# A decoder layer on one core: every engine's order written anew, one order over all engines, and norm rows stored once per partition

## The chip, the core and the metric

The kernel runs on one core of a Trainium2 chip. Five engines each work through a queue of their own, strictly in its order: PE (TensorE, matrix products), DVE (VectorE), ACT (ScalarE), POOL (GpSimd) and SP (SyncE, which here only issues transfers). An instruction that waits holds up everything behind it in its queue. The metric is device time in microseconds (us) of one execution. What a measurement of this kernel can tell from no change is about 0.2%, 1.64 us.

## The reference

One post-norm decoder layer for x of 512 tokens by 1024 channels, all in float32:

```python
h = x @ w_in                              # one projection, cut into 13 parts
y_a = nsa_attention(q, kc, vc, ks, vs, kw, vw, gates, ...) @ w_nsa_out
y_b = gated_deltanet(qkv, beta, decay, gate, ...) @ w_gdn_out
mix = (sigmoid(gate_a) * y_a + sigmoid(gate_b) * y_b) @ w_o
x = layer_norm(ALPHA * x + mix, ln1_g, ln1_b)
h = causal_dwconv(x @ w_up, conv_w)       # 2 x 2816 channels, width 3
gate, val = split(h)
x = layer_norm(ALPHA * x + (silu(gate) * val) @ w_down, ln2_g, ln2_b)
```

The attention has three branches (compressed blocks, the best eight of the selected blocks, a sliding window) with a gate each; the DeltaNet works in chunks of 64 tokens, with a triangular solve for each chunk. `layer_norm(x, g, b)` is `(x - mean) * rsqrt(var + eps) * g + b` over the 1024 channels.

## The kernel before, in words

**Products.** Float32 accuracy comes from splitting every operand in two: ACT (or DVE or POOL) makes a rounded copy, DVE (or POOL) the rest. A weight block arrives by a transfer as `raw`, becomes `wh` and `wl`, and every product is three matrix products into the same PSUM bank: hi by hi, lo by hi, hi by lo (lines L481, L483, L484; L1285 and L1449 are the same for the output projection and the FFN's second product, L536 to L538 for the token-major part of the first projection). A weight tile serves 128x512 outputs. `raw`, `wh` and `wl` have three buffers each, so a transfer can be issued only when an older block has been split.

**Stages.** Up to about 20 us PE makes the token-major projection `pb` out of x and its weights as they arrive (`xr`, `wB`). Then, to about 320 us, the other projections (`gps`) are mixed with attention (`aps`, `pout`) and DeltaNet (`dps`, the solve L769, L770, L772 on DVE). From there to 420 us come the two mixers' output projections, `pm0` and `pm1`: L1196 multiplies each by its gate `mt` (a tanh of a `gps`, L1118 on ACT), L1198 adds the two, and L1176, L1177 and L1210 to L1214 split the sum and make the sums of a two-by-two block product. To 460 us the projection `w_o` (L1285, into `pw` and `pu`), with L1290 adding it to x, L1249 and L1250 the norm, L1262 transposes. To about 715 us the FFN's up products (`pu`), the convolution (L1404, L1407) and the gate (L1411 to L1413), whose result is split into `ph` and `pl` (L1417, L1423, L1418, L1424) and added up in `sr` (L1425 to L1427). The down products (L1449) run to 812 us, as seven block products whose left sides are sums, copied by ACT to `hs` (L1443) and by DVE to `sl` (L1444). L1482 and L1486 take them off PSUM, then the norm again, and the result is sent out.

**Order.** `QUEUES` holds, for each engine, the numbers of its instructions as the program makes them, in the order in which they are to stand. `queues(tc)` walks each list and adds a scheduling dependency between neighbours on the same engine: no wait on the chip, only a place. Between engines nothing is fixed; the framework puts in what semaphores the data need, and which buffer or PSUM bank a rotating tile takes follows from the order in which it sees the instructions.

**Norm rows.** `layout` stacks the four rows g and b of both norms to 4 x 1024 (`lnr`). `rows_of(t, o)` at L1230 issues a transfer of two rows from SP into 128 partitions, reading the same 8 KB for each partition. `ln1` is read first by L1249 at 448 us, `ln2` at 792 us.

Of the kernel before, what the change touches and what calls it, by code (L numbers as in the profile page):

```python
# [19 lines left out]
D = 1024  # L20
# [50 lines left out]
def layout(a):  # L71
# [18 lines left out]
    for i in range(8):  # L90
# [28 lines left out]
        "lnr": np.stack([g("ln1_g")[0], g("ln1_b")[0], g("ln2_g")[0], g("ln2_b")[0]]),  # L119
# [207 lines left out]
77 81 87 90 110 78 71 84 72-73 70 93 85 74 92 94 86 82 91 95 111 144 96-97 83 98-99 79 100 106 101-102 89 103 112-130  # L327
132 131 133-137 147 150 138-139 142-143 145 153 148 146 149 151-152 154-155 157 156 158-161 163 162 165 164 166-171""",
    "SP": """0-7 17 8-9 15 25 10 12 11 13-14 19 18 16 20-24 26-75 80 79 81-82 78 83 77 84-85 76 86-134 136-165 167 135 169 171
173-180 170 166 182 168 172 181 183-184""",  # L330
}


# [1235 lines left out]
```

## Time and profile before

| | |
|---|---|
| time of three runs | 819.83, 820.98, 821.59 us; median 820.98 |
| span of the profiled execution | 820.8 us, mean granted PE clock 0.998 |
| busy: PE, DVE, ACT, POOL | 98%, 73%, 50%, 22% of the span |
| the chain that ended last | PE 79%, DVE 9%, DMA 7%, ACT 2%, issue 2% |
| the transfers of the norm rows | 2 of 1024 KB, issued at 429.6 and 775.4 us; issue to landing 9.6 and 6.7 us |

The page gives no time of its own for the profiled execution beside this span, which is 0.2 us under the median of the runs; sums that start at the span are therefore carried over to the median as they are. In a row of the timeline stand the start, the duration, the engine, the line, the operation, the tiles written and read, their shape, a count of like neighbours (xN), and in brackets the idle time before it and what ended it. Matrix products overlap, so that the step from one start to the next (0.223 us for 128x512 in steady stretches) says what one costs, not its duration.

### The profile page before, as it was taken

The numbers are of one execution on the slowest core, as the hardware profiler recorded it, in microseconds if no ns is written. First come the engines' busy times: TensorE is split into PE (matmuls) and PEld (weight loads), VectorE is DVE, ScalarE is ACT, GpSimd is POOL, SyncE is SP. The second block draws the span as 40 slices with busy tenths as digits, with TensorE's granted clock in tenths as the row PEclk, the third lists the DMA queues.
The fourth block names the chain that finished last, engine by engine and source line by source line (L and its number), as shares of the span: only waits on it lengthen the run. The fifth ranks groups of instructions, "written<-read, shape, count | busy, mean of one in ns | idle before, by whom it ended". The sixth has DMA issues, their size and how long they took to land.

```text
span 820.8 us, 11781 instructions
## 1 busy us (share of the span) xinstructions
PE 802.4 (98%) x4138; PEld 670.2 (82%) x4138; DVE 600.2 (73%) x1339; ACT 409.1 (50%) x912; POOL 179.7 (22%) x176
## 2 busy tenths in 40 slices
PE   8999999999999999999999999999999999999996
PEld 8788888787888888888787898888888888878784
DVE  5667689979768965556578956666685667777888
ACT  4453587774577764323254234344354444565641
POOL 0244835042365111241200101111111210200000
PEclk9999999999999999999999999999999999999999
DMA  8327280013624942343357387285336492465674
GB/s 282 106 78 267 80 267 30 26 53 97 161 86 103 194 90 77 108 134 123 103 209 226 129 168 243 93 185 146 98 117 210 111 235 91 143 202 178 210 220 149
DMA packets 43978, 119.57 MB, mean 146 GB/s; under 512 B 3472, under 2 KB 4624, under 8 KB 43664
## 3 DMA queue, kind: packets, MB, share of 16 engines
q1 hardware_dynamic: 32144, 87.37, 33.3%
q0 software_dynamic: 11776, 31.46, 16.6%
q8 instruction: 32, 0.52, 0.3%
q14 instruction: 26, 0.21, 0.1%
HBM read 116.72 MB, written 33.55 MB: 183 GB/s over the span
## 4 chain that ended last, share of the span: by engine, by line
PE 79%; DVE 9%; DMA 7%; ACT 2%; issue 2%; SPq 0%; POOL 0%; DVEq 0%; ACTq 0%; POOLq 0%
PE pu L481 9%; PE pu L483 9%; PE pu L484 9%; PE gps L481 9%; PE gps L483 8%; PE gps L484 8%; DMA raw<-wsum 3%; PE pout L1086 2%; PE aps L1072 2%; DMA raw<-in_down 2%; DVE wl L1385 2%; PE pz L1449 2%; PE pm L483 2%; PE pm L481 2%; PE pm L484 2%
## 5 line engine op out<-in xcount | busy, mean ns | idle before, releaser
L471 DVE TENSOR_TENSOR wl<-raw,wh 128x512 fp32r<-128x512 f32 x146 | 103.9, 717 | 73.2 <-ACT wh L467 40.9
L467 ACT ACTIVATE wh<-raw 128x512 fp32r<-128x512 f32 x126 | 79.0, 629 | 138.6 <-PE pu L483 91.4
L484 PE MATMUL pu<-mh,wl 128*128 128x512 f32 (+1 forms) x384 | 129.9, 372 | 0.2 <-DVE wl L471 0.2
L481 PE MATMUL pu<-mh,wh 128*128 128x512 f32 (+1 forms) x384 | 129.8, 372 | 0.0
L483 PE MATMUL pu<-ml,wh 128*128 128x512 f32 (+1 forms) x384 | 129.6, 372 | 0.0
L481 PE MATMUL gps<-xh,wh 128*128 128x512 f32 x320 | 123.5, 399 | 2.4 <-ACT mt L1118 1.5
L483 PE MATMUL gps<-xl,wh 128*128 128x512 f32 x320 | 123.2, 397 | 0.0
L484 PE MATMUL gps<-xh,wl 128*128 128x512 f32 x320 | 122.8, 397 | 0.0
L484 PEld LDWEIGHTS pu<-mh,wl 128*128 128x128 f32 x384 | 71.3, 188 | 13.4 <-DVE wl L471 0.6
L481 PEld LDWEIGHTS pu<-mh,wh 128*128 128x128 f32 x384 | 71.0, 188 | 12.6
L483 PEld LDWEIGHTS pu<-ml,wh 128*128 128x128 f32 x384 | 71.0, 188 | 12.6
L1407 DVE SCALAR_TENSOR_TENSOR fa<-pu,fcw,fa 128x511 f32<-128x511 f32 (+1 forms) x88 | 64.9, 745 | 18.9 <-ACT fa L1404 18.3
L1413 POOL TENSOR_TENSOR fth<-fth,fa 128x512 f32<-128x512 f32 x22 | 31.3, 1428 | 197.3 <-DVE fth L1412 182.8
L481 PEld LDWEIGHTS gps<-xh,wh 128*128 128x128 f32 x320 | 60.0, 188 | 13.5 <-issue 2.9
L484 PEld LDWEIGHTS gps<-xh,wl 128*128 128x128 f32 x320 | 60.0, 188 | 11.0 <-POOL wl L471 0.2
L483 PEld LDWEIGHTS gps<-xl,wh 128*128 128x128 f32 x320 | 60.1, 188 | 10.6
L1384 ACT ACTIVATE wh<-raw 128x512 fp32r<-128x512 f32 x67 | 40.0, 625 | 37.2 <-DMA raw<-wsum 11.4
L1385 DVE TENSOR_TENSOR wl<-raw,wh 128x512 fp32r<-128x512 f32 x67 | 44.5, 691 | 15.8 <-ACT wh L1384 15.3
L1404 ACT ACTIVATE fa<-pu,fcw 128x512 f32<-128x512 f32 x44 | 29.5, 681 | 30.7 <-PE pu L484 29.2
L471 POOL TENSOR_TENSOR wl<-raw,wh 128x512 fp32r<-128x512 f32 x30 | 40.0, 1337 | 13.5 <-ACT wh L467 7.1
L522 POOL TENSOR_TENSOR rs<-rs,minus_half 128x1 f32<-128x1 f32 x8 | 7.6, 949 | 155.9 <-DVE rs L1243 103.2
L1045 ACT ACTIVATE sc<-sc,mn 128x384 f32<-128x384 f32 (+2 forms) x64 | 35.6, 558 | 5.7 <-DVE mn L1043 5.2
(365 smaller groups left out, 1702.1 us busy)
## 6 DMA issues: line engine op xcount, KB each, us to landing
raw<-in_up SPq DMA_DIRECT2D x44, 512.0 KB, 3.7
raw<-in_wT SPq DMA_DIRECT2D x40, 512.0 KB, 3.5
wsum<-in_down POOLq DMA_DIRECT2D x6, 2816.0 KB, 21.7
raw<-wsum SPq DMA_DIRECT2D x20, 512.0 KB, 4.3
raw<-in_down SPq DMA_DIRECT2D x15, 512.0 KB, 3.9
osum<-in_wo POOLq DMA_DIRECT2D x6, 1024.0 KB, 9.4
wsum<-wsum POOLq DMA_DIRECT2D x2, 2816.0 KB, 14.2
raw<-in_wm SPq DMA_DIRECT2D x8, 512.0 KB, 3.5
```

Source lines behind the costliest of these rows:

```text
L467: A.activation(wh, r, AF.Copy)
L471: eng.tensor_tensor(wl, r, wh.bitcast(F32), op=OP.subtract)
L481: i = PE.matmul(ps, wh[k], mh_(k), start=(k == 0), stop=False)
L483: PE.matmul(ps, wh[k], ml_(k), start=False, stop=False)
L484: PE.matmul(ps, wl[k], mh_(k), start=False, stop=(k == n - 1))
L1045: A.activation(s[:, i, :n], s[:, i, :n], AF.Exp, scale=-1.0, bias=mn[:, 0, i:i + 1], accum_out=mn[:, 1, i:i + 1])
L1072: PE.transpose(pt[:, i, k, :], s[:, i, k * 128:(k + 1) * 128], ident)
L1384: A.activation(hi, raw[:, i], AF.Copy)
L1385: V.tensor_tensor(lo, raw[:, i], hi.bitcast(F32), op=OP.subtract)
L1404: A.activation(acc, ps, AF.Copy, scale=w[:, 2:3])
L1407: V.scalar_tensor_tensor(acc[:, n:], ps[:, :S - n], w[:, i:i + 1], acc[:, n:], op0=OP.mult, op1=OP.add)
L1413: G.tensor_tensor(th, th, g[1], op=OP.mult)
```

## The change

`lnr` is stored 128 times, once for each partition, and `rows_of` reads it so. All five lists in `QUEUES` are written anew. A string `TURNS` gives one order over all engines (P, D, A, G for POOL, S; a number repeats the letter), which `queues` adds as a second chain of scheduling dependencies. The instructions themselves are the same ones; most stand within 3 us of their old place, a few up to 12 us away. Through `TURNS` 577 of 1678 tiles take another buffer or PSUM bank than before.

```diff
+import re
...
-        "lnr": np.stack([g("ln1_g")[0], g("ln1_b")[0], g("ln2_g")[0], g("ln2_b")[0]]),
+        "lnr": np.broadcast_to(np.stack([g("ln1_g")[0], g("ln1_b")[0], g("ln2_g")[0], g("ln2_b")[0]]), (128, 4, 1024)),
...
 QUEUES = {
-    "PE": """0-9 11-12 10 13-32 41 38 35-37 33 42-43 53 39 34 54 44-45 47-48 40 50-52 46 49 59 62 55 63 65 56 64 60 66-67 61 57-58
...
+TURNS = """DS3P2SPS3DSADSASPDSP3ASP3ASDP2SDPAPSDP2DSP3SP2SP3SAP3SP2DPAP2ADP2DP3AP5DPAP2AP2DP3DPAP3APDP3APDP3AP3AP5DP2AP2DP3DP5DP3
...
 def queues(tc):
...
+    def chain(items):
+        for a, b in zip(items, items[1:]):
+            tc.add_manual_dep(b, a.name, mybir.DependencyInfo(
+                mybir.DependencyClass.NoSync, mybir.DependencyReason.SCHED_ONLY), reason="place in its queue")
+
+    rows = {}
     for k, runs in QUEUES.items():
-        last = None
-        for run in runs.split():
...
+        ends = [r.partition("-")[::2] for r in runs.split()]
+        rows[k] = [made[k][n] for a, b in ends for n in range(int(a), int(b or a) + 1)]
+        chain(rows[k])
+    names = {"G" if k == "Pool" else k[0]: iter(r) for k, r in rows.items()}
+    chain([next(names[x]) for x, n in re.findall(r"([A-Z])(\d*)", TURNS) for _ in range(int(n or 1))])
...
     def rows_of(t, o):
-        nc.sync.dma_start(out=t, in_=bass.AP(tensor=d["lnr"].tensor, offset=d["lnr"].offset + o * D,
-                                             ap=[[0, 128], [D, 2], [1, D]]))
+        nc.sync.dma_start(out=t, in_=d["lnr"][:, o:o + 2, :])
```

Lines from 332 on of the old file stand 54 or 55 further down in the new one: L1285 is L1339 there, L484 is L539, L1182 is L1237. Three places show the kind of move.

**PE at about 395 us** (old clock): the end of a pair `pm0`, `pm1`, then the gate product `gps_4659` that takes the PSUM bank of an older gate product. Before:

```order
L481 MATMUL gps_4566<-xh_93,wh_4562 128x512
L484 MATMUL pm0_4603<-yoh_4005,wl_4597 128x512
L483 MATMUL gps_4566<-xl_94,wh_4562 128x512
L484 MATMUL pm1_4617<-yoh_4005,wl_4601 128x512
L484 MATMUL gps_4566<-xh_93,wl_4564 128x512
L481 MATMUL gps_4566<-xh_93,wh_4562 128x512
L483 MATMUL gps_4566<-xl_94,wh_4562 128x512
L484 MATMUL gps_4566<-xh_93,wl_4564 128x512
L481 MATMUL gps_4659<-xh_93,wh_4651 128x512
```

Now:

```order
L539 MATMUL pm1_4617<-yoh_4005,wl_4601 128x512
L538 MATMUL gps_4566<-xl_94,wh_4562 128x512
L539 MATMUL gps_4566<-xh_93,wl_4564 128x512
L536 MATMUL gps_4566<-xh_93,wh_4562 128x512
L538 MATMUL gps_4566<-xl_94,wh_4562 128x512
L539 MATMUL gps_4566<-xh_93,wl_4564 128x512
L536 MATMUL gps_4566<-xh_93,wh_4562 128x512
L538 MATMUL gps_4566<-xl_94,wh_4562 128x512
L539 MATMUL gps_4566<-xh_93,wl_4564 128x512
L536 MATMUL gps_4566<-xh_93,wh_4562 128x512
L538 MATMUL gps_4566<-xl_94,wh_4562 128x512
L539 MATMUL gps_4566<-xh_93,wl_4564 128x512
```

The pair is finished first; eleven products of `gps_4566` now stand between its last product and `gps_4659` (the next row), where four stood.

**PE at about 419 us:** the end of the last pair, and the first product into `pu1_4886`, which may start only when DVE has read both `pm` banks (L1196). Before:

```order
L484 MATMUL pm1_4792<-yoh_4005,wl_4776 128x512
L1285 MATMUL pw1_4858<-woh_4209,mh_3997 128x512
L1285 MATMUL pw0_4857<-woh_4209,mh_3997 128x512
L484 MATMUL pm0_4778<-yoh_4005,wl_4772 128x512
L1285 MATMUL pw0_4857<-wol_4210,mh_3997 128x512
L1285 MATMUL pw1_4858<-wol_4210,mh_3997 128x512
L1285 MATMUL pw0_4857<-woh_4209,ml_3998 128x512
L1285 MATMUL pw0_4857<-woh_4209,mh_3997 128x512
L1285 MATMUL pw1_4858<-woh_4209,ml_3998 128x512
L1285 MATMUL pu1_4886<-woh_4390,mh_3997 128x512
```

Now:

```order
L1339 MATMUL pw1_4858<-woh_4209,mh_3997 128x512
L536 MATMUL pm1_4792<-yoh_4005,wh_4774 128x512
L538 MATMUL pm1_4792<-yol_4036,wh_4774 128x512
L539 MATMUL pm0_4778<-yoh_4005,wl_4772 128x512
L539 MATMUL pm1_4792<-yoh_4005,wl_4776 128x512
L1339 MATMUL pu1_4886<-woh_4390,mh_3997 128x512
L1339 MATMUL pu1_4886<-wol_4391,mh_3997 128x512
L1339 MATMUL pu1_4886<-woh_4390,ml_3998 128x512
L1339 MATMUL pu0_4885<-woh_4390,mh_3997 128x512
```

Between the last product of `pm1_4792` and the first of `pu1_4886` stood eight products; now none. On DVE both L1196 (first that of `pm1_4792`, then that of `pm0_4778`) still stand in this order.

**ACT at about 325 us:** the copies `yoh` of both mixers' results, and the first weight block `wh_4114` of the first pair `pm0`. Before:

```order
L1182 ACTIVATE yoh_4005<-oT_3216 128x512
L1182 ACTIVATE yoh_4005<-yT_1416 128x512
L1118 ACTIVATE mt_3974<-gps_3949 128x512
L1182 ACTIVATE yoh_4005<-oT_1504 128x512
L1182 ACTIVATE yoh_4005<-oT_2255 128x512
L467 ACTIVATE wh_4114<-raw_4112 128x512
L467 ACTIVATE wh_4118<-raw_4112 128x512
```

Now:

```order
L1237 ACTIVATE yoh_4005<-oT_3216 128x512
L1237 ACTIVATE yoh_4005<-oT_1504 128x512
L1237 ACTIVATE yoh_4005<-yT_2131 128x512
L1173 ACTIVATE mt_3974<-gps_3949 128x512
L1237 ACTIVATE yoh_4005<-oT_2255 128x512
L1237 ACTIVATE yoh_4005<-yT_1416 128x512
L1237 ACTIVATE yoh_4005<-oT_3700 128x512
L1237 ACTIVATE yoh_4005<-yT_2629 128x512
L522 ACTIVATE wh_4114<-raw_4112 128x512
```

Three more copies stand ahead of the weight block; on PE its first product `pm0_4122` has moved ahead of four products of `gps` that stood before it.

On SP the transfer of `ln1` has moved behind the next three weight blocks (`raw_5045`, `raw_5063`, `raw_5099`), that of `ln2` behind the next two (`raw_7920`, `raw_7950`); at the start the small constants stand behind the blocks of x and `wB`, and `xr5` stands before `xr7`, `wB3` and `xr6`.

More of the change, by code (lines that the diff above doesn't have):

```diff
@@ L328 @@
[L328 to L331 removed]
+    "PE": """0-2 11 14 17-18 15 12 8 3-4 19 9 29 10 5 13 30 20-21 23 6 16 24 22 26-28 7 31 25 35 38 41 32 42 39 36 33 43 34 37
+53-54 44 47 45 40 46 55 50 65 51-52 48-49 59 66 56 60 57 62-63 58 68 64 74 61 67 77 75 71 69 76 72-73 78-79 70 80-81
@@ new lines @@
+3748 3735 3739-3740 3752 3741 3749 3737 3745 3753 3750 3746 3757 3747 3754 3738 3755 3742 3758 3756 3743 3760 3744
+3759 3763 3761-3762 3766 3764-3765 3769-3771 3775-3777 3767 3781 3768 3782 3772 3783 3787 3773-3774 3778 3788
+3779-3780 3784-3786 3790 3789 3791-3793 3796-3798 3802-3806 3794 3807 3795 3799-3801 3808-3821 3847 3822-3828
+3848-3851 3829-3831 3852-3854 3832 3855 3833-3835 3856 3836-3837 3857 3838-3839 3858 3840-3846 3859-3879""",
+    "DVE": """0-2 4-5 3 7 6 9 8 10-15 17 16 18 58-59 19 60-61 20 27 21-23 64 25 90 66 31-32 65 33-41 62 42-43 67 44-45 63 46-47 72
@@ new lines @@
+1231 1236 1218 1237 1222 1220 1240-1241 1228 1232 1224 1242 1223 1233 1243 1238 1248 1225 1244 1249-1250 1229 1245
+1251-1252 1254 1246 1253 1239 1255 1234 1256-1257 1235 1258 1247 1259-1262 1265 1263-1264 1266-1270 1273 1271-1272
+1274""",
+    "Activation": """0-1 3-4 2 5-6 8 7 10 9 12 11 15 14 13 16-17 20 23 26 24 21 27 22 18-19 28 31 25 30 33 41 34-36 42-45 37 32 38-40 51 46
+61 52-53 29 62 54-55 47-48 67 49 68 56 50 57 82 58 63 59 64-65 83 66 60 69-72 84-85 73-75 110 93 76-77 80 111 94 103
@@ new lines @@
+696 691-692 703 705 700 706 693 707 711 699 712-713 704 714-716 718 717 719 709 720 708 721 723-724 701 726-727 729
+731 710 732 730 722 728 725 733-734 739 735 737-738 736 740-741 744 743 746 745 747 742 749 748 751-752 754-755
+757-758 750 759-760 762-763 761 756 765-766 753 769 768 772 767 771 773 770 774-775 764 777 776 778-792 794 793
+795-798""",
+    "Pool": """8 10 9 11-13 3-6 15 7 16 0 17 141 19-22 27-28 1 33 105 25 23 34 29 107 39 36 30 2 31-32 14 40 18 24 43 38 37 44 26 41
+108 54 45 48 35 55 42 51 49 47 52 66 64-65 68 46 62 67 57 69 50 58 56 140 53 59 61 63 75-76 60 80 77 90 78 81 86 109
@@ L340, in queues @@
             made[k].append(i)
-    for k, runs in QUEUES.items():
-        last = None
-        for run in runs.split():
-            a, _, b = run.partition("-")
-            for n in range(int(a), int(b or a) + 1):
-                i = made[k][n]
-                if last is not None:
-                    tc.add_manual_dep(i, last.name, mybir.DependencyInfo(
-                        mybir.DependencyClass.NoSync, mybir.DependencyReason.SCHED_ONLY), reason="place in its queue")
-                last = i
+    def chain(items):
[3 more added lines that the diff above has]
+    rows = {}
+    for k, runs in QUEUES.items():
+        ends = [r.partition("-")[::2] for r in runs.split()]
[3 more added lines that the diff above has]
+    chain([next(names[x]) for x, n in re.findall(r"([A-Z])(\d*)", TURNS) for _ in range(int(n or 1))])
 @with_exitstack
```

418 lines of the change are left out of this document (228 added, 190 removed), and 3 rows, old and new, of the table QUEUES.

## The prediction, made before the change was timed

> **What bounds the kernel now.** First the page's totals and its chain of the work that ended last:
>
> ```profile
> span 820.8 us, 11781 instructions
> PE 802.4 (98%) x4138; PEld 670.2 (82%) x4138; DVE 600.2 (73%) x1339; ACT 409.1 (50%) x912; POOL 179.7 (22%) x176
> PE 79%; DVE 9%; DMA 7%; ACT 2%; issue 2%; SPq 0%; POOL 0%; DVEq 0%; ACTq 0%; POOLq 0%
> ```
>
> PE bounds it, and the change gives PE the same products. What can be won is the time in which PE stands, so the waits of PE come next (line, releaser, us in all, times, longest), then two stretches by engine:
>
> ```profile
> PE gps L481 <- ACT mt L1118: 1.5, 1, 1.5
> PE dps L656 <- DVE z L772: 1.1, 1, 1.1
> PE aps L1072 <- DVE sc L1056: 0.8, 1, 0.8
> PE pb L536 <- ACT xh L447: 0.8, 1, 0.8
> PE dps L736 <- DVE yT L892: 0.7, 1, 0.7
> PE pu L1285 <- DVE x L1290: 0.7, 1, 0.7
> PE pu L1449 <- DVE wl L1385: 0.5, 1, 0.5
> PE pw L1285 <- DVE x L1290: 0.2, 1, 0.2
> PE pu L484 <- DVE wl L471: 0.2, 1, 0.2
> ...
> 143.50:164.00 20.50, 18.58 (x126) 15.36 (x125) 19.61 (x84) 15.85 (x44) 0.59 (x2) 1.00 0.09 26
> ...
> 554.04:574.54 20.50, 20.50 (x92) 16.98 (x91) 14.12 (x23) 8.44 (x14) 3.52 (x3) 1.00 0.53 146
> ```
>
> These nine kinds are 6.5 us. The FFN's stretch shows the other extreme: 92 products in 20.50 us, one every 0.223 us, with nothing to win; I take 0.223 us for a product everywhere. The columns after the length are PE, weight loads, DVE, ACT, POOL, clock, transfers. From 143.5 to 164 us DVE is busy 19.61 of 20.50 us: there an order can win little. So the question at each of these places is what the new order puts between the cause and the waiting product, and then whether it makes new ones.
>
> **What goes.** The largest wait, at 397.79, in the timeline of PE, DVE and ACT:
>
> ```profile
> 395.03 0.39 PE L484 MATMUL pm<-yoh,wl 128*128 128x512 f32 x1
> ...
> 395.00 1.29 DVE L1196 SCALAR_TENSOR_TENSOR mt<-mt,pm 128x512 f32<-128x512 f32 x2 [3.18 <-PE pm L484]
> 396.32 0.69 DVE L1198 TENSOR_TENSOR mt<-mt 128x512 f32<-128x512 f32 x1
> ...
> 397.05 0.60 ACT L1118 ACTIVATE mt<-gps 128x512 f32<-128x512 f32 x1 [7.86 <-DVE mt L1198]
> ...
> 397.79 0.47 PE L481 MATMUL gps<-xh,wh 128*128 128x512 f32 x1 [1.47 <-ACT mt L1118]
> ```
>
> From the start of the pair's last product to `gps_4659` the chain PE, DVE twice, DVE, ACT takes 397.79 - 395.03 = 2.76 us. Before, that product and the four behind it cover 5 x 0.223 = 1.12 us: 1.64 lost. Now eleven follow: 12 x 0.223 = 2.68, and 0.08 is left. On ACT a weight copy (`woh`) and a split (`ah`, of ACT's other inputs) now stand ahead of this `mt`, but ACT had been idle 7.86 us, so I take **-1.5**; bounds -1.6 and, if one copy as long as the 0.60 of `mt` gets in the way, -0.9.
>
> At the start PE waits for x:
>
> ```profile
> 8.52 5.58 DMA xr<-in_xT
> ...
> 13.42 1.33 ACT L447 ACTIVATE xh<-xr 128x512 fp32r<-128x512 f32 x2 [1.27 <-DMA xr<-in_xT]
> ...
> 14.80 0.53 PE L536 MATMUL pb<-wh,xh 128*128 128x288 f32 x2 [0.77 <-ACT xh L447]
> ```
>
> The transfers are what runs here. `xr5`, issued at 8.52, is waited for until 14.10, and ACT's two copies start at 13.42 with that of `xr6`, which is of no use before its weights. Now `xr5` stands in `xr6`'s place, 14.10 - 13.42 or 0.7 us earlier, and the small constants are behind it: this wait is mostly gone, **-0.8**; bounds -1.2 (what comes after it arrives sooner too) and 0.
>
> Before, eight warm-up products stand ahead of all work; now three do, the others between the first real ones. The Trainium skill, "TensorE: Matmul & The Clock Gate", Part 1, speaks against that: whatever is issued in about the first 3.4 us of sustained activity runs at half speed. By it the start could give back the 0.8 it wins; the time would be 821.1, still no change. No run here shows a start with fewer warm-up products, and the sum goes by the rows.
>
> At 155 and 158.9 (1.9 us idle) DVE ends a triangular solve:
>
> ```profile
> 157.32 0.17 DVE L769 TENSOR_TENSOR tmp<-lx,xs 128x8 f32<-128x8 f32 x1
> ...
> 157.52 0.17 DVE L770 TENSOR_TENSOR xs<-xs,tmp 128x8 f32<-128x8 f32 x1
> ```
>
> Operations on 8 elements step by 0.20 us since each needs the one before. In the old order the last eight follow one another; now `L1043`, `L1076`, `L1047` and others stand between them, and nine `gps` products move behind the transposes that wait at 155. The work ahead of `z` is the same, so of 1.9 I take **-1.2**; bounds 0 (DVE is as good as full) and -2.2.
>
> Smaller: `yT` at 193 (0.7) no longer has a weight cast and a split (L1076) ahead of it on DVE: **-0.6**, bounds 0 and -0.9. The waits for `x` at 440 and 445 (0.9) get 8 and 7 products in front, 1.8 and 1.6 us, but DVE is what is late there, and its queue to L1250 is as long as before: **-0.4**, bounds 0 and -1.2. `wl` at 500 (0.2) gets five products in front: **-0.2**. What goes: 1.5 + 0.8 + 1.2 + 0.6 + 0.4 + 0.2 = 4.7 us.
>
> **What comes.** At 419 the new order does the reverse of 395:
>
> ```profile
> 419.22 0.39 PE L484 MATMUL pm<-yoh,wl 128*128 128x512 f32 x1
> ...
> 419.64 1.37 DVE L1196 SCALAR_TENSOR_TENSOR mt<-mt,pm 128x512 f32<-128x512 f32 x2 [0.95 <-PE pm L484]
> ...
> 421.25 0.40 PE L1285 MATMUL pu<-woh,mh 128*128 128x512 f32 x1
> ```
>
> DVE can read `pm1` 0.42 after its last product starts, and both L1196 take to 1.79 after it. Before, eight products lie between, 9 x 0.223 = 2.01: covered. Now `pu1_4886` comes 0.22 after it and waits 1.79 - 0.22 = 1.57, and all of PE behind it. DVE has 0.95 idle ahead, so nothing makes it earlier: **+1.55**, bounds +1.3 and +1.8.
>
> At 329:
>
> ```profile
> 324.80 0.63 ACT L1182 ACTIVATE yoh<-oT 128x512 fp32r<-128x512 f32 x1 [2.14 <-DVE yT L892]
> ...
> 326.34 1.14 ACT L1182 ACTIVATE yoh<-oT 128x512 fp32r<-128x512 f32 x2
> 327.38 1.30 ACT L467 ACTIVATE wh<-raw 128x512 fp32r<-128x512 f32 x2
> ...
> 329.44 0.39 PE L481 MATMUL pm<-yoh,wh 128*128 128x512 f32 x1
> ```
>
> `wh_4114` is done at about 328.0, 1.44 before its product. Three more copies at 0.52 (326.34 to 327.38 for two) make it 1.56 later, and four products fewer ahead make PE come 0.89 earlier: 1.56 + 0.89 - 1.44 = **+1.0**; bounds +0.2 (if `yT`, for which the first copy waits, comes sooner) and +1.3.
>
> At 727 and 733 ACT's copies `hs` move ahead of the weights:
>
> ```profile
> 726.97 0.50 PE L1449 MATMUL pu<-wl,ph 128*128 128x512 f32 x1 [0.51 <-DVE wl L1385]
> ...
> 729.82 1.06 ACT L1443 ACTIVATE hs<-sr 128x1024 fp32r<-128x1024 f32 x1 [2.26 <-DVE sr L1427]
> 730.79 0.61 ACT L1384 ACTIVATE wh<-raw 128x512 fp32r<-128x512 f32 x1
> 731.31 0.83 ACT L1443 ACTIVATE hs<-sr 128x768 fp32r<-128x768 f32 x1
> ...
> 733.32 0.70 PE L1449 MATMUL pz<-wh,hs 128*128 128x512 f32 x2 [0.16 <-ACT wh L1384]
> ```
>
> Ahead of `wh_7479` stood `hs` of 0.97 and 0.73; now 0.97, 0.73, 0.97 and 0.97: 1.94 later. Against it PE has two products more in front (0.45), and POOL's product, for which DVE's chain to `hs` waited, comes earlier, as its tanh (L1411) has moved before three copies: some 0.4. The old waits here (0.51 and 0.16) are then part of the new one, 0.67 + 1.94 - 0.45 - 0.4 = 1.76: **+1.1**; bounds -0.6 (both go) and +1.5.
>
> For the many small moves in the FFN, where sums (L1419, L1425) now stand ahead of some `wl` that PE takes just in time, I allow two waits like the 0.2 of the row `PE pu L484 <- DVE wl L471`: an estimate, **+0.4**, bounds 0 and +1.2. What comes: 1.55 + 1.0 + 1.1 + 0.4 = 4.05 us.
>
> **The norm rows.**
>
> ```profile
> ln<-in_lnr SPq DMA_DIRECT2D x1, 1024.0 KB, 9.6
> ...
> 439.20 0.36 SPq L1168 DMA_DIRECT2D raw<-osum  x1
> ...
> 448.11 1.42 DVE L1249 SCALAR_TENSOR_TENSOR x<-x,mv,ln 128x512 f32<-128x512 f32 x2
> ...
> ln<-in_lnr SPq DMA_DIRECT2D x1, 1024.0 KB, 6.7
> ```
>
> Nobody waits for them now. `ln1` now follows the issue at 439.20, so at 439.6, and L1249 wants it at 448.1, or about 447 if the waits at 440 and 445 go. By the 6.7 us of `ln2` it lands at 446.3: in time. By the 9.6 of `ln1` itself at 449.2: 2 us late. The new layout can only change how the source is read; neither row shows that apart. The blocks that `ln1` shared the transfers with are now ahead of it and mostly landed, so I take **0**, by the shorter row; bounds 0 and +3. `ln2` moves behind two blocks in the same way and gets the same 0.
>
> **The sum:** 820.8 - 4.7 + 4.05 = 820.15 of span, a gain of 0.65; from the median 820.98 about **820.3**. The tail after the last product keeps its chain to the output and isn't touched.
>
> **The rivals.** *Faster:* the new waits at 329 and 733 and the allowance don't come, since ACT's copies slide forward into the idle time ahead of them (2.14 and 2.26 in the rows above); then 820.98 - 4.7 + 1.55 = 817.8, and with the waits at 155 and 193 gone whole 816.5. For it: ACT is at 50%. Against: both idle times end on an event of DVE that the new order leaves where it was. *Slower:* the norm rows. If `ln1` takes over 7.4 us it lands after 447; then L1249 holds DVE, and behind it stand the transposes' input (L1250) and the split of the next weights. At 9.6 it is 2.2 late, and the splitting that L1249 holds up (L1172, on twice the width of the 0.69 rows, about 1.2) comes on top: 820.3 + 2.2 + 1.2 = 823.7. *All moves are hidden:* the old waits stay, since what is late is DVE and not its order, and nothing new comes: 821.0. For it speaks the full DVE at 155; against it the wait at 397.79, behind an idle DVE (3.18) and an idle ACT.
>
> **How the numbers follow.** Gains and new waits cancel 0.38, all hidden 0.08, faster 0.35, slower 0.19 (0.14 norm rows, 0.05 a wait that I have not seen). What a measurement can tell from no change is 0.2% or 1.64 us, so the first two are "same", 819.3 to 822.6; the likeliest has a range of its own from 819.3 to 822.2. For 8 in 10 the low end goes into the faster case, to 816.3, just past its full form, and the high end to 822.9, which holds a late `ln1` up to about 9 us without what comes on top.
>
> **What would show it.** Right: no wait of `gps` on `mt` L1118 at about 394; a new one of about 1.5 us of `pu` on DVE L1196 (now L1251) near 418, the first of `pm` on ACT `wh` near 327, `pz` or `pu` waiting 1 us or more on ACT near 731. Wrong: those missing while the old ones are gone (faster), or DVE waiting on `ln` near 446 (slower), or PE at half clock after 6 us. The old waits standing unchanged would mean that I misread what order decides here.

## The result and the profile after

The changed kernel takes **831.71 us** (median of four runs, 830.46 to 832.33), the kernel before in the same session 820.79 (four runs, 819.83 to 821.59): a ratio of 1.0128, 95% interval 1.0114 to 1.0143. It is **slower by 10.9 us**, outside the forecast range, and on the side that I gave 0.19.

The totals of the changed kernel's page, which answer to the first fence of the prediction:

```profile
span 828.7 us, 11773 instructions
PE 806.1 (97%) x4138; PEld 671.2 (81%) x4138; DVE 606.9 (73%) x1339; ACT 409.9 (49%) x912; POOL 182.0 (22%) x176
```

PE does the same products. DVE does the same operations too, yet is busy 606.9 us where it was 600.2: some operations became longer. The waits of PE in the changed kernel (line, releaser, us in all, times, longest):

```profile
PE dps L817 <- DVE gx L815: 2.2, 2, 1.5
PE pu L1339 <- DVE mt L1251: 1.5, 1, 1.5
PE gps L609 <- DVE vm L606: 1.4, 1, 1.4
PE pm L536 <- ACT wh L522: 1.1, 1, 1.1
PE pb L591 <- ACT xh L502: 1.1, 1, 1.1
PE gps L536 <- issue: 1.0, 1, 1.0
PE gps L536 <- DVE acc L697: 0.9, 1, 0.9
PE dps L711 <- DVE vraw L707: 0.9, 1, 0.9
PE pz L1503 <- ACT wh L1438: 0.9, 1, 0.9
PE pu L1503 <- ACT wh L1438: 0.8, 1, 0.8
PE pw L1339 <- DVE mv L1295: 0.7, 1, 0.7
...
```

Rows two, four and nine are the three waits that I forecast (419, 329, 733); the wait on `mt` L1118 near 394 is gone, as forecast. Row ten belongs to the wait at 733 too. What I had not foreseen are the first row and those on `acc` and `vraw`, all on DVE, and that PE now waits for `xh` at 4.2 us (row five).

To see where time goes I use **PE's standing time**: the start of a product less the sum of the steps of all products that ran before it, each form of product at its step in steady stretches (0.227 us for 128x512), the same for all kernels. The 0.223 used up to the prediction is a little low: of the 92 products counted in that stretch two had started before it. The table gives it after so many us of products, worked out from the traces. The kernel before is shown by the run E1 below, which has its order:

| us of products done | 10 | 70 | 130 | 160 | 200 | 250 | 310 | 380 | 400 | 450 | 620 | 710 | 780 |
|---|---|---|---|---|---|---|---|---|---|---|---|---|---|
| order before (E1) | 5.1 | 7.3 | 9.7 | 14.0 | 16.7 | 18.6 | 20.2 | 22.0 | 22.0 | 22.8 | 23.6 | 24.4 | 25.1 |
| changed | 6.2 | 8.4 | 16.1 | 18.3 | 19.2 | 23.7 | 27.8 | 27.8 | 29.9 | 31.6 | 32.5 | 35.3 | 35.6 |
| changed, old norm rows (E2) | 5.1 | 7.2 | 15.0 | 17.7 | 18.5 | 24.6 | 28.6 | 28.6 | 30.6 | 32.5 | 33.4 | 35.3 | 37.1 |
| new order at 60-148 only (E5) | 4.5 | 6.6 | 14.3 | 18.6 | 21.2 | 23.1 | 24.8 | 26.5 | 26.5 | 28.3 | 29.1 | 29.7 | 30.2 |
| changed, 13 POOL fills (E9) | 5.4 | 7.5 | 11.9 | 14.6 | 15.4 | 17.8 | 21.9 | 21.8 | 23.9 | 26.0 | 26.8 | 28.9 | 30.2 |
| all causes away (E14) | 5.6 | 7.7 | 11.0 | 13.2 | 14.1 | 16.4 | 19.0 | 19.9 | 20.1 | 21.9 | 22.7 | 24.7 | 25.9 |

The largest step is between 70 and 130: 7.7 us against 2.4. The next is that before 250. Two places of the changed kernel's timeline show what they have in common (start, duration, engine, line, operation, tiles, shape):

```profile
78.02 1.63 POOL L526 TENSOR_TENSOR wl<-raw,wh 128x512 fp32r<-128x512 f32 x1 [5.20 <-PE gps L539]
78.43 1.28 DVE L824 TENSOR_TENSOR tmp<-lx,xs 128x36 f32<-128x36 f32 x1
...
87.11 1.28 POOL L695 TENSOR_TENSOR acc<-acc,tap 128x509 f32<-128x509 f32 x1 [0.44 <-ACT tap L694]
87.19 1.23 DVE L824 TENSOR_TENSOR tmp<-lx,xs 128x4 f32<-128x4 f32 x1
88.45 0.17 DVE L825 TENSOR_TENSOR xs<-xs,tmp 128x4 f32<-128x4 f32 x1
...
266.63 0.69 POOL L555 DMA_DIRECT2D osum<-osum  x1
266.80 2.40 DVE L1108 TENSOR_TENSOR mn<-mn,gsig 128x1 f32<-128x1 f32 x1
267.33 1.30 POOL L526 TENSOR_TENSOR wl<-raw,wh 128x512 fp32r<-128x512 f32 x1
268.55 0.62 POOL L524 CAST wh<-raw 128x512 fp32r<-128x512 f32 x1
269.12 0.74 DVE L815 TENSOR_TENSOR gx<-f,cst 128x256 fp32r<-128x256 f32 x2
269.58 0.38 PE L817 MATMUL dps<-gx,same_r 128*128 128x256 f32 x1 [1.47 <-DVE gx L815]
```

A product of one element per partition takes 2.40 us. The view of this tile's operations by line (count, then shortest, median and longest in ns) says what it takes otherwise:

```profile
L1108 DVE TENSOR_TENSOR mn<-mn,gsig x30: 140/155/2395, 114.6 to 314.1; 128x1 f32<-128x1 f32 x30
```

It ends when POOL's cast ends (269.17), and `dps`, the first row of the waits, is late by it. At 87 a product of four elements takes 1.23, until POOL's sum ends. These operations don't wait for a result of POOL. **They are held while POOL works**, and no row of idle time shows it: the hold is inside the duration. Counting DVE operations over 0.2 us longer than the median of their line and shape in the kernel before: 25 with 15.4 us too much before, 29 with 23.3 us in the changed kernel.

### The profile page after: what moved, and what is told of

It reads as the page before. It is cut to its first block, busy times and chain, and to the rows that moved or that the text cites. A ratio compares the mean times of both kernels' runs of the same rounds, so it can differ in the third digit from the quotient of the medians.

```text
span 828.7 us, 11773 instructions
## 1 busy us (share of the span) xinstructions
PE 806.1 (97%) x4138; PEld 671.2 (81%) x4138; DVE 606.9 (73%) x1339; ACT 409.9 (49%) x912; POOL 182.0 (22%) x176
## 3 DMA queue, kind: packets, MB, share of 16 engines
q0 software_dynamic: 11776, 31.46, 16.7%
## 4 chain that ended last, share of the span: by engine, by line
PE 82%; DVE 10%; DMA 3%; ACT 2%; issue 2%; POOL 0%; DVEq 0%; SPq 0%; ACTq 0%; POOLq 0%
PE pu L539 10%; PE pu L538 10%; PE pu L536 10%; PE gps L538 8%; PE gps L536 8%; PE gps L539 8%; PE px L1503 4%; PE pz L1503 3%; PE pout L1141 2%; PE aps L1127 2%; PE pm L536 2%; PE pm L538 2%; PE pm L539 2%; PE dps L711 1%; DMA raw<-wsum 1%
## 5 line engine op out<-in xcount | busy, mean ns | idle before, releaser
L526 DVE TENSOR_TENSOR wl<-raw,wh 128x512 fp32r<-128x512 f32 x146 | 105.7, 727 | 72.7 <-ACT wh L522 31.1
L536 PE MATMUL pu<-mh,wh 128*128 128x512 f32 (+1 forms) x384 | 131.7, 372 | 0.0
L539 PE MATMUL pu<-mh,wl 128*128 128x512 f32 (+1 forms) x384 | 129.2, 372 | 0.5 <-DVE wl L526 0.5
L536 PE MATMUL gps<-xh,wh 128*128 128x512 f32 x320 | 126.6, 404 | 2.0 <-issue 1.0
L539 PE MATMUL gps<-xh,wl 128*128 128x512 f32 x320 | 126.2, 403 | 0.2 <-DVE wl L526 0.2
L538 PE MATMUL gps<-xl,wh 128*128 128x512 f32 x320 | 126.1, 401 | 0.0
L539 PEld LDWEIGHTS pu<-mh,wl 128*128 128x128 f32 x384 | 71.0, 188 | 13.5 <-DVE wl L526 0.9
L539 PEld LDWEIGHTS gps<-xh,wl 128*128 128x128 f32 x320 | 60.2, 188 | 10.6 <-DVE wl L526 0.6
L1439 DVE TENSOR_TENSOR wl<-raw,wh 128x512 fp32r<-128x512 f32 x67 | 45.1, 699 | 14.5 <-ACT wh L1438 13.9
L526 POOL TENSOR_TENSOR wl<-raw,wh 128x512 fp32r<-128x512 f32 x30 | 40.4, 1347 | 18.5 <-PE gps L539 8.6
L1458 ACT ACTIVATE fa<-pu,fcw 128x512 f32<-128x512 f32 x44 | 29.6, 681 | 24.8 <-PE pu L539 24.6
L1100 ACT ACTIVATE sc<-sc,mn 128x384 f32<-128x384 f32 (+2 forms) x64 | 35.6, 558 | 11.5 <-DVE mn L1098 10.1
## 6 DMA issues: line engine op xcount, KB each, us to landing
wsum<-in_down POOLq DMA_DIRECT2D x6, 2816.0 KB, 23.3
```

The source lines that it names most:

```text
L526: eng.tensor_tensor(wl, r, wh.bitcast(F32), op=OP.subtract)
L536: i = PE.matmul(ps, wh[k], mh_(k), start=(k == 0), stop=False)
L538: PE.matmul(ps, wh[k], ml_(k), start=False, stop=False)
L539: PE.matmul(ps, wl[k], mh_(k), start=False, stop=(k == n - 1))
L1100: A.activation(s[:, i, :n], s[:, i, :n], AF.Exp, scale=-1.0, bias=mn[:, 0, i:i + 1], accum_out=mn[:, 1, i:i + 1])
L1439: V.tensor_tensor(lo, raw[:, i], hi.bitcast(F32), op=OP.subtract)
```

## The experiments

Kernels with a mixed order are made from one list of all instructions of all engines, cut at a product of PE and spliced: inside a stretch the order of one kernel, outside that of the other. All times of stretches are on the clock of the kernel before. Kernels that are mostly of the old order have the new norm rows, which E1 shows to be free (E6 has the old ones). Ratios are to the kernel before on the same chip, with 95% intervals.

**E1 and E2: the two parts of the change apart.** E1 is the kernel before with the norm rows stored and read the new way, E2 the changed kernel with them the old way:

```diff
-        nc.sync.dma_start(out=t, in_=bass.AP(tensor=d["lnr"].tensor, offset=d["lnr"].offset + o * D,
-                                             ap=[[0, 128], [D, 2], [1, D]]))
+        nc.sync.dma_start(out=t, in_=d["lnr"][:, o:o + 2, :])
```

> The kernel before with one part of the change: the norm rows stored once per partition and read so; every order stays. Of the changed kernel's 10.9 us, 7.9 are in the span of the profiled execution and the rest seems to lie outside it (its time was 830.46 at a span of 828.7). Theory A (the new layout costs time outside the span, a larger input, or the same time in the transfers): the median is 1.5 to 2.5 us above the kernel before. Theory B (the layout is free, all of the loss is in the orders): within 0.6 us of the kernel before; then what lies outside the span is there in the kernel before too.

> The changed kernel with the old norm rows: the new orders alone. Theory A (the layout costs about 2 us): 829.5 to 830.0 against 831.7 of the changed kernel. Theory B (all of it is the orders): 831.0 to 832.4, that is 10.3 to 11.5 us above the kernel before.

E1: 820.47 us, 0.9998 (0.9989 to 1.0008). E2: 831.50, 1.0121 (1.0103 to 1.0140). Theory B: the layout is free, all of the loss is in the orders. E1 also corrects my base. Its page says

```profile
span 818.0 us, 11781 instructions
```

at the same median and the same order as the kernel before, whose profiled execution had a span of 820.8. So a span is about 2 us short of the time, and the execution that I had worked from was some 3 us longer than E1's, with waits for `x` near 440 that E1's list of waits does not have. Near 440, though, E1 is the exception: the traces of E3, E5, E6, E11 and E12, which have the old order there, show waits for `x` of 0.4 to 0.7 us. The median was the right base, but not for the reason that I gave.

**E3 and E4: are the gains the order's own?** The order before, with the new one only at 148 to 222 us (E3), and also at 385 to 412, 426 to 444 and 738 to 775 (E4):

```diff
- order of the kernel before
+ order of the kernel before, the new order's inside 148-222 [E4: and 385-412, 426-444, 738-775]
```

> The order before, with the new order (of all engines) only for the work that stood between 148 and 222 us. In the two traces PE's standing time is 6.3 us more in the changed kernel at 140 us of products done and only 2.25 more at 200: it won 4 us there. Theory A (these are the gains that the new order was forecast to bring, at 155 and 193): the kernel is 3 to 4.5 us faster than before, 816.5 to 818. Theory B (payback: PE came 6 us late into a stretch in which DVE is full and was already ahead, so the waits that DVE sets there shrank by themselves): within 1 us of the kernel before, 820 to 821.8.

> The order before, with the new order only in the four stretches in which the changed kernel won against the kernel before: 148 to 222, 385 to 412, 426 to 444 and 738 to 775 us. By the two traces: -4.1, -1.7, -1.0 and -0.9. Theory A (the gains are the order's own): -6 to -8, 813 to 815. Theory B (the first is payback): only the others remain, -2.5 to -3.6, 817.2 to 818.5. If the gain at 395 that I predicted (1.5) is not the order's own either, 819 or more.

E3: 818.97, 0.9979 (0.9970 to 0.9988): -1.7 us, between the theories. Its list of waits from 146 to 166 us shows why:

```profile
PE aps L1124 <- DVE sc L1108: 1.6, 1, 1.6
PE aps L1091 <- DVE mn L1095: 0.4, 1, 0.4
```

In E1 there stand in the same window:

```profile
PE dps L656 <- DVE z L772: 1.1, 1, 1.1
PE aps L1072 <- DVE sc L1056: 0.8, 1, 0.8
```

At 155 nothing is won, the wait stands a little earlier: standing time between 130 and 160 us of products is 4.5 us against 4.3. The changed kernel needs only 2.2 there, since its PE comes in 6 us late. What the order wins itself is between 170 and 200: 0.6 against 2.5. E4: 818.44, 0.9970 (0.9959 to 0.9982), -2.2 where A said at least -6 and B at least -2.5, so it is near B: at 380 us of products it wins 1.7, of which 0.6 are lost again before 390; at 430 it loses 1.2 more than E1 (E3, with the old order there, loses 1.0 more than E1 too), and the stretch at 738 gives nothing.

**E5: the loss between 60 and 148 us alone.**

```diff
- order of the kernel before
+ order of the kernel before, the new order's inside 60-148
```

> The order before, with the new order only for the work that stood between 60 and 148 us, where the changed kernel loses 5.2 us (PE's standing time between 60 and 130 us of products done: 2.9 before, 8.2 now), which I did not foresee. Theory A (what is lost there is lost): 825 to 826. Theory B (payback: behind it DVE is full and sets PE's waits, so a PE that comes 5 us late waits less there, and the standing time between 130 and 200 us of products, 7.0 before, falls to about 4.3): the loss is again 5 at 130 and the kernel ends 2 to 3 us above the kernel before, 822.5 to 824.

825.49, 1.0050 (1.0032 to 1.0067): theory A by the median. The interval, 2.6 to 5.5 us, doesn't rule out B; the trace does. From 70 to 130 it loses the same 7.7, and between 130 and 200 it still waits 7.0 us: nothing is paid back. The smaller waits of the changed kernel there need both, a late PE and the new order.

**E6 and E7: does POOL hold DVE?** In both kernels POOL's operations are replaced by fills of the same tiles in the same places (the exponentiation of POOL stays). Left out are the products, sums, splits and copies that POOL made:

```diff
+        def tensor_tensor(self, o, a, b, op):
+            if op == OP.pow:
+                return nc.gpsimd.tensor_tensor(o, a, b, op=op)
+            return nc.gpsimd.memset(o.bitcast(F32) if o.dtype == F32R else o, 0.01)
+        def tensor_copy(self, o, a):
+            return nc.gpsimd.memset(o.bitcast(F32) if o.dtype == F32R else o, 0.01)
```

> The kernel before, in which POOL's element by element operations and copies are replaced by fills with a constant of the same tile in the same place of POOL's queue: POOL writes, but reads no SBUF, and is done sooner; the products of two tiles, the sums and the splits that POOL makes are left out, so the output is not the reference's. Theory A (DVE is held while a POOL operation that reads SBUF runs): the 25 DVE operations that take over 0.2 us longer than their like (15.4 us together) become fewer than 8. The kernel before suffers little from them: 816 to 820. Theory B (the long DVE operations have another cause, a transfer or a wait inside the operation): they stay, and the time is within 2 us of the kernel before.

> The changed kernel with the same replacement of POOL's operations by fills (the same work left out). Theory A (in the new order DVE operations on PE's path fall behind the start of a POOL operation at 78, 87, 102 to 110, 141 and 267 us, and that is what makes the unforeseen waits): the 29 long DVE operations (23.3 us) go, the standing time between 60 and 130 us of products falls from 8.2 to at most 5, the step at 250 us of products (2.3 and 3.9 in two runs) to under 1, and the kernel comes within 3 to 5 us of the same kernel with the order before. Theory B (the new order itself is late there, whatever POOL does): the distance stays at 8 to 11 us.

E6: 817.84, 0.9959 (0.9946 to 0.9972); long DVE operations 7 instead of 25, 2.4 us too much instead of 15.4. E7: 825.60, 1.0053 (1.0036 to 1.0070); 3 instead of 30 (as in E2), 1.5 us instead of 24.0. Their number of operations is the same, and DVE's busy time in E7 is

```profile
PE 804.1 (98%) x4138; PEld 672.9 (82%) x4138; DVE 584.5 (71%) x1339; ACT 409.2 (50%) x912; POOL 104.9 (13%) x176
```

that is 22.4 us less than in the changed kernel, without one operation of DVE changed. The holds are POOL's. The long operations that stay in E6 and E7 are casts, copies and products with a scalar, 0.2 to 0.75 us too long beside a fill or a transfer issue of POOL. The distance between the two kernels is 7.8 us, though, where A said 3 to 5 and B 8 to 11: by the time alone B is nearer. The trace of E7 shows what spoiled the comparison: at 68 us a block of weights is there 4.5 us later than in E2, and PE stands 4.5 us more there, which E6 does not have. Without it some 3.3 would be left; why the block is late stays open. The step at 250 is gone (0.1). E6 also serves as a control: between 70 and 130 and at 250 its PE stands as long as E1's, to 0.1 us, so that in the old order the fills win nothing at these places.

**E9: only the operations in question.** The changed kernel with 13 fills, 11 of POOL's operations between 76 and 110 us and two at 266.6 to 268.5; those 13 results are left out:

```diff
+    FILL = {18, 23, 25, 27, 28, 33, 34, 39, 40, 43, 44, 97, 98}
...
+                if me in FILL:
+                    return nc.gpsimd.memset(o.bitcast(F32) if o.dtype == F32R else o, 0.01)
```

> The changed kernel in which only 13 POOL operations are replaced by fills that read nothing: eleven between 76 and 110 us (splits of weights, one sum of a convolution, z, at, grh, grl) and the split and cast at 266.6 to 268.5 us; their results are left out, so the output is not the reference's. Nothing on DVE, ACT or PE waits for these eleven in the trace, so that they end sooner helps nobody. Theory A (DVE held behind a reading POOL operation makes the unforeseen waits): the DVE operations held at 78, 87, 88, 102, 104, 108 and 109 us and the 2.4 us one at 267 take their usual time; the one at 141 us, behind a POOL sum that stays, is held as before; PE's standing time between 70 and 130 us of products falls from 7.7 to 3 to 4.5, the step at 250 us of products from 2.3 to 3.9 to under 1; time 824.5 to 827. Theory B (the order itself is late there): 70 to 130 stays over 6.5, 250 over 2, time over 829.

825.43, 1.0059 (1.0038 to 1.0080), **6.3 us less than the changed kernel** by the medians, 5.7 by the ratios. From 70 to 130 PE stands 4.4 us instead of 7.7, at 250 0.2 instead of 2.3 to 3.9, all as A said. In its timeline near 263 the same small product (L1122 here) takes its usual time, beside the same issue of a transfer and a fill:

```profile
262.92 0.68 POOL L422 DMA_DIRECT2D osum<-osum  x1
263.06 0.16 DVE L1122 TENSOR_TENSOR mn<-mn,gsig 128x1 f32<-128x1 f32 x1
263.14 0.75 DVE L829 TENSOR_TENSOR gx<-f,cst 128x256 fp32r<-128x256 f32 x2
263.58 0.56 POOL L421 MEMSET wl<- 128x512 f32 x1
```

and the operation that I left alone is held as before, behind a sum of POOL:

```profile
137.01 1.44 POOL L422 TENSOR_TENSOR acc<-acc,tap 128x511 f32<-128x511 f32 x1 [1.71 <-ACT tap L708]
137.23 1.77 DVE L829 TENSOR_TENSOR gx<-f,cst 128x512 fp32r<-128x512 f32 x1
```

The Trainium skill, "SBUF — State Buffer", section "Who interferes with whom", states this: a VectorE operation with two inputs in SBUF and a GpSimd operation that reads SBUF need the same read port, and whichever is issued second is blocked until the first has ended; one that only writes does not block it. The trace agrees: the forms `acc<-gps,tiny,acc` and `sc<-aps,cst`, which take one input from PSUM, are never held in E2, no operation on two SBUF tiles is held beside a fill, and held are operations on two SBUF tiles and, as the same section has it for two-port modes, casts and products with a scalar. I had not weighed that rule. One row doesn't show the order of the rule: the 2.40 us operation starts by the profile at 266.80, 0.53 us before the POOL split that holds it (267.33), beside a transfer issue which in E9 holds nothing.

**E8: the two forecast waits at 329 and 419 put back** in the changed kernel:

```diff
- PE: pm1_4792 (last), pu1_4886
+ PE: pm1_4792 (last), eight products of pw0_4857 and pw1_4858, pu1_4886
- all engines, 324.5-333 us: new order
+ all engines, 324.5-333 us: order before
```

> The changed kernel with two places put back: the eight products that lay between the last product into pm1 and the first into pu1 near 419 us, and the order of all engines around ACT's copies into yoh at 325 us. These are the two waits that I predicted at +1.55 and +1.0 and that the trace of the changed kernel shows at 1.70 and 1.28. If the new order is what makes them, PE's standing time loses 2.0 at 400 us of products and 1.5 to 1.7 at 310, and the kernel is at 827.5 to 828.6 (against 831.5 to 831.7). If it is lateness of DVE and ACT that only shows up elsewhere (payback), 829.5 or more.

830.23, 1.0099 (1.0086 to 1.0113): -1.5 us by the medians, -2.4 by the ratios. That is over the 829.5 from which I had expected lateness that only shows up elsewhere. The trace says more. The wait near 421 goes (0.25 of the 2.0 left at 400). Of the 1.7 near 329 only 0.55 go: a wait of `pm` on `wh` of 0.4 stands 4 us later. So the first is the order's own, the second partly.

**E10: three more losses put back** in the changed kernel, the order before inside three stretches:

```diff
- new order
+ new order, the order before inside 256-276, 604-618, 726-748
```

> The changed kernel with the order before put back in three stretches (all engines): 256 to 276, 604 to 618 and 726 to 748 us of the old clock. In the two traces the changed kernel loses there 2.3 to 3.9, 0.8 and 1.7 us. Theory A (each loss is made where it shows, by the order of these few us): -4 to -6, 825.5 to 828. Theory B (lateness brought along from earlier): under -2, over 829.5. The forecast wait of pz and pu on ACT near 733, told at +1.1, goes in A with at least 1.5.

831.97, 1.0141 (1.0125 to 1.0157): nothing won, so by the time theory B. The step at 250 falls to 0.1 though a wait of 0.8 stands just ahead of it, and that at 690 to 710 from 2.9 to 1.6, much as A has it; but at the edge of the middle stretch there is a new wait of `pu` on a split of weights, 2.5 us by the list of waits, and the standing time grows by 4.4 at 600. Here the splice made a worse order than both, so the run does not say whether these losses can be had back.

**E11 and E12: only what gains.** The order before with the new one at 165 to 222 and 385 to 412 us (E11), in E12 also at 492 to 512:

```diff
- order of the kernel before
+ order of the kernel before, the new order's inside 165-222, 385-412 [E12: and 492-512]
```

> The order before with the new order only in two stretches: 165 to 222 us, without the solve at 148 to 165 in which the wait only stood elsewhere, and 385 to 412 us, the place of the forecast -1.5. The gains of the two add up if they are the orders' own: -1.6 and -1.7, 817 to 818.2 against 820.7 to 821.4 of the kernel before. If the first one needs the order from 148 on, 819 or more.

> The same with the new order also from 492 to 512 us, where I forecast -0.2 for the wait on wl at 500 and the traces of the two kernels differ by 0.45: PE's standing time at 480 us of products is 0.45 lower than in the same kernel without it, and the median 0.3 to 0.6 lower, which is less than the two medians can tell apart; the trace decides.

E11: 818.17, 0.9967 (0.9957 to 0.9978). E12: **817.71, 0.9963 (0.9951 to 0.9975)**, with 0.1 instead of 0.45 at 480 us of products. Both beat both kernels by more than the intervals; they compute all that the kernel before computes. The gains at 193 and 395 are the orders' own. In E11 they come to 2.5 us by the medians, of the 3.3 that the traces had given, as behind the second one 0.6 is lost again before 390 us of products, as in E4.

**E13 and E14: is there more?** E13 keeps the new order but for the five blamed stretches; E14 is E9 with two more fills (the convolution sums before 141 us; 15 results left out), the two places of E8 and the order before at 726 to 748:

```diff
- new order
+ new order, the order before inside 60-148, 256-276, 318-335, 410-428, 690-748
```

```diff
-    FILL = {18, 23, 25, 27, 28, 33, 34, 39, 40, 43, 44, 97, 98}
+    FILL = {18, 23, 25, 27, 28, 33, 34, 39, 40, 43, 44, 51, 52, 97, 98}
- new order
+ new order, the places of E8 and 726-748 as before
```

> The new order everywhere but in the five stretches that the runs so far blame, which have the order before again: 60 to 148, 256 to 276, 318 to 335, 410 to 428 and 690 to 748 us of the old clock (all engines). Theory A (the loss of 10.9 us is made in these five and nowhere else, and the gains at 180 to 200 and 395 stay): 817.5 to 820, slower than the two gaining stretches alone (818.2, 817.7) by at most the waits for x near 440 (0.85) and on the split near 650 (0.8). Theory B (part of the loss is spread over the whole order, such as buffers that the one order over all engines gives out otherwise): over 822.

> The changed kernel with everything that is blamed taken away together, the held operations by fills and not by another order: POOL's 13 fills of before and two more (the convolution sums before 141 us; the results of all 15 are left out), the places at 329 and 421 us put back, and the order before from 726 to 748 us. If the pieces add up: 825.4 less 1.4 (329 and 421), 0.9 (141) and 1.2 to 1.7 (733), so 821.4 to 822. If the waits come back elsewhere as PE gets earlier, 823 or more.

E13: 826.37, 1.0066 (1.0048 to 1.0083): not theory A, and over 822, as B has it. But its trace shows holds that neither kernel has, at the edge of a stretch:

```profile
268.49 1.29 POOL L794 TENSOR_TENSOR at<-at,cst 128x512 f32<-128x512 f32 x1
268.69 1.17 DVE L823 TENSOR_TENSOR tmp<-lx,xs 128x60 f32<-128x60 f32 x1
...
270.42 1.26 POOL L525 TENSOR_TENSOR wl<-raw,wh 128x512 fp32r<-128x512 f32 x1
270.55 1.21 DVE L823 TENSOR_TENSOR tmp<-lx,xs 128x56 f32<-128x56 f32 x1
```

They cost PE 2.1 us at 260 us of products, the wait at 140 is 2.9, the one that E3 has, and at 760 to 775 PE stands 2.0 us (1.8 in E2, nothing in E1). So E13 does not decide between the two theories. E14: 821.70, 1.0005 (0.9993 to 1.0017), as the sum of the pieces said: **with the named causes away the new order is level with the old one as it stands**. An old order without its own holds would be faster, too: E6, with nearly all of POOL's reads away, is 3.4 us ahead of it. That the new order is not ahead by its gains is due to what stays: against E1 its trace loses 0.5 at the start, 0.9 near 440 (where E1 is the exception), 0.8 near 650, 1.2 near 733 and 0.85 at the last products. These were not taken away one by one.

## Why the prediction was wrong

Each term, as the difference of the standing time of the changed kernel and E1 over its stretch:

| stretch | forecast | measured | what the runs show |
|---|---|---|---|
| start | -0.8 | +0.95 (mean of 8 new and 8 old starts: 5.75 and 4.80 at 10 us; single ones 5.1 to 6.4 and 4.4 to 5.4) | wrong sign |
| 70 to 130, `acc`, `wl`, `vraw` | 0 | +5.3 | held DVE operations, not seen: 3.3 go with the fills of E9, 1.1 more in E14, 0.9 stay open |
| 155/159, the solve | -1.2 | -2.1, but +0.2 alone (E3) | the wait moves; gain only behind a late PE |
| 193, `yT`, and around | -0.6 | -1.85, also alone (E3) | right sign, a third of the size; what the rest is was not traced |
| 250, `gx` | 0 | +2.3 and +3.9 (E2) | one held operation; not seen |
| 329 | +1.0 | +1.7 | right, too small |
| 395/397 | -1.5 | -1.7; alone (E4) 0.6 of it is lost again right behind | right |
| 419 | +1.55 | +2.0 | right |
| 440/445, `x` | -0.4 | +0.85 | no gain: from 410 to 450 the changed kernel stands 1.7, E3, E5, E6, E11 and E12 with the old order 1.7 to 2.0, and E1 alone 1.0 |
| 500, `wl` | -0.2 | -0.45, also alone (E12) | right |
| FFN | +0.4 | +0.8 | `wl` near 650, held behind POOL (1.77 us instead of 0.69) |
| 733 | +1.1 | +1.35 | right |
| norm rows | 0 | 0 (E1) | right |

The step that failed is the one for **DVE's and POOL's durations**: I took every operation at its duration in the kernel before and let the order move only what waits for what. The terms that I had come to +1.6 instead of -0.65, the two that I had put at 0 without a reason to +7.6 (9.2 with E2's step at 250). The rows make 9.2 of the 10.5 us by which the two traces differ at 780 us of products; the rest lies between the stretches. The mechanism of the three new waits and of the gains at 193, 395 and 500 was right, and together with the norm rows they come out near the forecast (+1.05 instead of +1.35). The missing term was the holds. Three smaller terms failed too, the start, the solve and `x`; that the solve's -2.1 goes beyond the forecast is luck, since it takes a late PE. The list of waits in the prediction also leaves out five rows of that view, 3.5 us; one of them, `pb` on `wh` (0.7), the new order does remove. The chance of 0.05 that I gave to "a wait I have not seen" was far too small for an order made anew on five engines.

The rows for the forecast waits have the forecast form. At 419 `pu` stands right behind the last product of the pair (the second of the two in the first row):

```profile
425.57 0.61 PE L539 MATMUL pm<-yoh,wl 128*128 128x512 f32 x2
426.29 1.28 DVE L1251 SCALAR_TENSOR_TENSOR mt<-mt,pm 128x512 f32<-128x512 f32 x2 [1.95 <-PE pm L539]
427.72 0.47 PE L1339 MATMUL pu<-woh,mh 128*128 128x512 f32 x1 [1.54 <-DVE mt L1251]
```

The wait is 1.54; I had forecast 1.55. At 733 `hs` runs ahead of `wh`:

```profile
737.35 2.75 ACT L1497 ACTIVATE hs<-sr 128x1024 fp32r<-128x1024 f32 x3 [1.84 <-DVE sr L1481]
740.00 1.14 ACT L1438 ACTIVATE wh<-raw 128x512 fp32r<-128x512 f32 x2
741.04 1.04 ACT L1497 ACTIVATE hs<-sr 128x1024 fp32r<-128x1024 f32 x1
741.99 1.66 ACT L1438 ACTIVATE wh<-raw 128x512 fp32r<-128x512 f32 x3
742.75 0.70 PE L1503 MATMUL pz<-wh,hs 128*128 128x512 f32 x2 [0.85 <-ACT wh L1438]
```

At the **start** the wait for `x` at 14.80 is gone, but E1 doesn't have it either, and in the changed kernel the products run at half pace for longer. In E1 the warm-up products run without a gap and the step of the 128x288 products falls from 0.24 to 0.13 us at 6.3 us:

```profile
1.45 3.78 PE L554 MATMUL gps<-vm 128*128 128x128 f32 x16 [1.45 <-DVE vm L551]
5.27 0.44 PE L537 MATMUL pb<-wl,xh 128*128 128x288 f32 x1
5.51 0.44 PE L536 MATMUL pb<-wh,xh 128*128 128x288 f32 x1
...
6.39 0.29 PE L537 MATMUL pb<-wl,xh 128*128 128x288 f32 x1
6.52 0.30 PE L538 MATMUL pb<-wh,xl 128*128 128x288 f32 x1
```

In the changed kernel PE stands after the first few, and the step is still 0.24 at 8.6 us:

```profile
1.43 1.65 PE L609 MATMUL gps<-vm 128*128 128x128 f32 x6 [1.43 <-DVE vm L606]
4.20 1.20 PE L591 MATMUL pb<-wh,xh 128*128 128x288 f32 x3 [1.11 <-ACT xh L502]
...
8.63 0.44 PE L592 MATMUL pb<-wl,xh 128*128 128x288 f32 x1
8.87 0.44 PE L591 MATMUL pb<-wh,xh 128*128 128x288 f32 x1
```

In E2, with the same order, it is down to 0.13 by 7.5 us. The granted clock of the profile is 1.00 from 8 to 10 us of the changed kernel, so that the half pace, one of my signs of being wrong, shows in the steps alone. It is what the rule which I cited ("TensorE: Matmul & The Clock Gate" of the Trainium skill, Part 1) speaks of. The trace agrees with it in direction, though half pace lasts longer here than the rule's 3.4 us: 4.8 us from the first product in E1. I set it aside because no row showed it, and took the gain instead. No run undid the start alone, so that the slow products are the whole of the 0.95 is argued, not shown.

Of the rivals, *slower* had the right side by the wrong mechanism: nothing ever waited for the norm rows. *Faster* rested on ACT sliding forward; the waits at 329 and 733 came instead.

## What to carry to other kernels

Before judging an order by waits, compare each operation's duration with the median of its line and shape: a hold behind another engine hides inside a busy row, and an order that is better by dependencies can lose more by where two-input DVE operations meet POOL's reads. A change that moves everything should be split by stretches of time and only the winning ones kept: two or three short stretches here are worth 2.5 to 3 us, the whole order costs 10.9. The places where stretches are joined make holds and waits of their own (E10, E13). And one profiled execution is not the kernel: a wait of under 1 us is a term only if a second trace has it.

## What the hardware did that I had not expected

A DVE operation of 0.15 us can be held for 2.25 us: it did not get in between two POOL operations that follow each other (267.33 to 268.63 and 268.55 to 269.17 above). Not every meeting is a hold, and the rows tell which is. In E2 26 DVE operations that make a rounded 128x512 tile of two inputs start inside a POOL operation, transfer issues aside. Nine take over 0.2 us longer: both inputs are in SBUF, 0.39 to 1.27 us of the POOL operation are left, and each ends 0.55 or 0.56 us after it, as in the rows of E9 above (POOL to 138.45, DVE to 139.00). Of the other 17, nine take one input from PSUM and three meet POOL's exponentiation of 4 or 1 elements per partition. Five start with at most 0.22 us left; four of them also end 0.55 us after POOL, which makes them at most 0.08 us longer, and one takes its usual 0.69. So in this trace such an operation ends 0.55 us after POOL's or when it would anyway, whichever is later. POOL can be the one held, too: in the kernel before a split of DVE that starts at 711.57 takes its usual time inside a product of POOL of 2.56 us, which elsewhere takes 1.28 to 1.76.

Holds are very regular from run to run: those at 78, 87, 102, 104, 108 and 110 us are in the changed kernel, E2, E5, E8 and E10 within 0.02 us of the same length: in these runs the order of the queues fixes them.
